# Gate and up of a SwiGLU layer, token-stationary, with a fast matrix product on part of the contraction

## The chip, the core and the metric

The kernel runs on one core of a Trainium2 chip. Five engines work side by side, each through its own queue of instructions in order: TensorE (PE, matrix products), VectorE (DVE), ScalarE (ACT), GpSimd (POOL) and SyncE (SP, which issues the weight transfers here). The metric is the device time of one execution, in microseconds (us).

## What is computed

A decoder trunk of two layers over 256 tokens (2 token tiles of 128) with a model width of 2048 (16 k-tiles of 128). Each layer has a mixer of three head groups, which the change doesn't touch, and a SwiGLU feed-forward part (FFN) of width 5632 = 44 x 128:

```python
def rms_norm(x, w):
    y = xf * lax.rsqrt(jnp.mean(xf * xf, axis=-1, keepdims=True) + NORM_EPS)
    return (y * w.astype(jnp.float32)).astype(x.dtype)

def swiglu(h, w_gate, w_up, w_down):
    return (jax.nn.silu(h @ w_gate) * (h @ w_up)) @ w_down

for l in range(DEPTH):
    h = rms_norm(x, mix_norm_w[l])
    x = x + hybrid_mixer(h, ...)
    h = rms_norm(x, ffn_norm_w[l])
    x = x + swiglu(h, w_gate[l], w_up[l], w_down[l])
return rms_norm(x, final_norm_w)
```

All data are float32.

## The kernel before

**Products in three parts.** Every float32 operand is split into a high part (rounded to the matmul's own format) and the rest, the low part. A product a x b is then three matmuls: high x high, high x low and low x high. For a weight tile, `unit` (lines 125 to 136) does it: SP brings a unit of 128 x 1024 values (512 KB) into one of three `raw` buffers, ACT writes the high part `whi` (line 134), DVE subtracts it from the raw values to give `wlo` (line 135). `whi` and `wlo` have four buffers each. The activations lie transposed as x^T: `hs[k]` holds for k-tile k a tile `hl` of 512 columns, 256 tokens high and 256 tokens low.

**Two forms of a product.** `block_a` (line 162) holds the weights still and moves the tokens: for each k-tile one matmul of `whi` against all 512 columns of `hl`, then one of `wlo` against the 256 high columns. The result is transposed (FFN column by token) and sits in two halves that `evac_a` (line 178) adds. `block_b` (line 186) holds a token tile still and moves 512 weight columns: three matmuls of 512 columns for each k-tile and token tile.

**The FFN** (`ffn`, line 804). It runs in three parts of 16, 16 and 12 tiles of 128 FFN columns (`FF_PARTS`). For each tile f `block_a` computes gate (`pg`) and up (`pu`); ACT and DVE join the halves, multiply both by `rb` (the row of 1/rms of each token, broadcast over the partitions), take Silu and multiply (lines 815 to 820); the result is split into `hid` high and low. After the tiles of a part `block_b` runs the down product (`dn`) over that part's tiles for each of four groups of 512 output columns, and `add_x` adds it to x. In the last part each finished group of columns starts what comes next (`nxt.piece`): the transposes of x and their split for the next layer's mixer, or the squares and weights of the final norm, which ends with `Final.last` for one token tile after the other. x^T is not scaled before the products: 1/rms is applied to the result, so the first products needn't wait for it.

**What sets the order.** A scheduler of the framework places each engine's instructions by its own timeline; tiles from a pool with n buffers wait until an old one is free. PSUM, where products end, has 8 banks of 512 columns: four for `dps` (tag "d"), two for tag "m" and two for "mg". The DVE row for weights is the plainest piece of it:

```python
act.activation(out=whi[:, c], in_=raw[:, c], func=AF.Copy)
dve.tensor_tensor(out=wlo[:, c], in0=raw[:, c], in1=f32(whi[:, c]), op=SUB)
```

Of the kernel before, what the change touches and what calls it, by code (L numbers as in the profile page):

```python
# [58 lines left out]
def tile_trunk(ctx: ExitStack, tc: tile.TileContext, x: bass.AP, wu: bass.AP, prm: bass.AP,  # L59
               cst: bass.AP, fnw: bass.AP, out: bass.AP, depth: int, units: list):  # L60
    nc = tc.nc
# [116 lines left out]
    def evac_a(ps, dst, rb, scale=None):  # L178
        act.copy(out=dst, in_=ps[:, S:])  # L179
        dve.tensor_tensor(out=dst, in0=ps[:, :S], in1=dst, op=ADD)  # L180
        if scale is None:
            dve.tensor_tensor(out=dst, in0=dst, in1=rb, op=MUL)
        else:
            dve.scalar_tensor_tensor(out=dst, in0=dst, scalar=scale, in1=rb, op0=MUL, op1=MUL)
# [617 lines left out]
            dve.tensor_tensor(out=xc, in0=pst[t][:, :w], in1=xc, op=ADD)  # L802

    def ffn(l, norm, nxt):
        hs = norm.hs
        rb = None
        f0 = 0
        for part, nf in enumerate(FF_PARTS):
            fs = []
            for f in range(f0, f0 + nf):  # L810
                pg, pu = dps("pg"), dps("pu")
                block_a(l, (("gate", f * P, pg), ("up", f * P, pu)), hs)
                if rb is None:
                    rstd, rb = norm.scale()
                ga = sp.tile([P, S], F32, tag="ac", name="ga", bufs=2)
                evac_a(pg, ga, rb)
                act.activation(out=ga, in_=ga, func=AF.Silu)
                up = sp.tile([P, S], F32, tag="tz", name="up", bufs=2)
                evac_a(pu, up, rb)
                dve.tensor_tensor(out=up, in0=up, in1=ga, op=MUL)  # L820
                if f % 2 == 0:
                    hid = g4("hid", [2, 2, S], F32R, "gg" if part % 2 else "gy")
                hi, lo = hid[:, 0, f % 2], hid[:, 1, f % 2]
                act.activation(out=hi, in_=up, func=AF.Copy)  # L824
                dve.tensor_tensor(out=lo, in0=up, in1=f32(hi), op=SUB)  # L825
                fs.append((hi, lo))
# [101 lines left out]
```

## Time and profile before

| | us |
|---|---|
| median of 3 runs (2394.24 to 2395.49) | 2394.96 |
| the profiled execution | 2394.46 |
| its span, first to last instruction | 2392.7 |
| PE busy | 2377.5 (99%) |
| DVE busy | 1498.8 (63%) |
| ACT busy | 1197.6 (50%) |
| POOL busy | 75.7 (3%) |

The profile is of one execution; its times are compared with that execution's own 2394.46 us. Matmuls are pipelined: the next begins before the record of the last ends, so the pitch from one to the next, not the mean duration, says what one costs. The chain that ended last is followed back from the last instruction, at each step to what released it.

### The profile page before, as it was taken

The numbers are of one execution on the slowest core, as the hardware profiler recorded it, in microseconds if no ns is written. First come the engines' busy times: TensorE is split into PE (matmuls) and PEld (weight loads), VectorE is DVE, ScalarE is ACT, GpSimd is POOL, SyncE is SP. The second block draws the span as 40 slices with busy tenths as digits, with TensorE's granted clock in tenths as the row PEclk, the third lists the DMA queues.
The fourth block names the chain that finished last, engine by engine and source line by source line (L and its number), as shares of the span: only waits on it lengthen the run. The fifth ranks groups of instructions, "written<-read, shape, count | busy, mean of one in ns | idle before, by whom it ended". The sixth has DMA issues, their size and how long they took to land.

```text
span 2392.7 us, 34536 instructions
## 1 busy us (share of the span) xinstructions
PE 2377.5 (99%) x13300; PEld 2075.5 (87%) x13300; DVE 1498.8 (63%) x2354; ACT 1197.6 (50%) x1875; POOL 75.7 (3%) x107
## 2 busy tenths in 40 slices
PE   8999999999999999999999999999999999999998
PEld 7888888888888888888898888889888888888887
DVE  5898655566655665466658976565666556655665
ACT  5754455555434454444567545555554344544544
POOL 0220000000000000000003100000000000000000
PEclk9999999999999999999999999999999999999999
DMA  6555445455565555556555544454656655566564
GB/s 214 174 176 167 136 159 187 162 191 195 194 195 176 196 192 197 189 178 197 190 172 184 176 145 155 159 185 160 196 194 196 194 177 189 196 206 194 184 202 159
DMA packets 120886, 436.06 MB, mean 182 GB/s; under 512 B 13584, under 2 KB 14480, under 8 KB 120720
## 3 DMA queue, kind: packets, MB, share of 16 engines
q1 hardware_dynamic: 120160, 432.70, 55.5%
q8 instruction: 104, 1.70, 0.3%
q10 hardware_dynamic: 560, 1.15, 0.1%
q14 instruction: 62, 0.51, 0.1%
HBM read 431.70 MB, written 2.10 MB: 181 GB/s over the span
## 4 chain that ended last, share of the span: by engine, by line
PE 98%; DMA 1%; ACT 1%; DVE 0%; issue 0%; POOLq 0%; POOL 0%; DVEq 0%; ACTq 0%
PE pu L69 20%; PE pg L69 20%; PE dn L69 20%; PE wo L69 7%; PE fq L69 4%; PE fk L69 4%; PE fv L69 4%; PE gkq L69 3%; PE mq L69 2%; PE mk L69 2%; PE gvp L69 2%; PE gz L69 2%; PE mv L69 2%; PE mo L69 1%; PE fs L69 1%; PE mog L69 1%
## 5 line engine op out<-in xcount | busy, mean ns | idle before, releaser
L135 DVE TENSOR_TENSOR wlo<-raw,whi 128x1024 fp32r<-128x1024 f32 (+2 forms) x821 | 991.0, 1218 | 658.8 <-ACT whi L134 432.1
L134 ACT ACTIVATE whi<-raw 128x1024 fp32r<-128x1024 f32 (+2 forms) x821 | 866.4, 1056 | 869.5 <-DMA raw<-wu 448.5
L69 PE MATMUL dn<-whi,hid 128*128 128x512 f32 (+1 forms) x1504 | 440.6, 376 | 0.0
L69 PE MATMUL pu<-hl,whi 128*128 128x512 f32 x1408 | 350.2, 391 | 0.0
L69 PE MATMUL pg<-hl,whi 128*128 128x512 f32 x1408 | 336.9, 391 | 0.0
L69 PEld LDWEIGHTS dn<-whi,hid 128*128 128x128 f32 x1504 | 276.2, 188 | 50.6
L69 PEld LDWEIGHTS pu<-hl,whi 128*128 128x128 f32 x1408 | 259.0, 188 | 50.3
L69 PEld LDWEIGHTS pg<-hl,whi 128*128 128x128 f32 x1408 | 259.0, 188 | 50.2
L69 PE MATMUL dn<-wlo,hid 128*128 128x512 f32 (+1 forms) x752 | 282.6, 376 | 0.0
L69 PEld LDWEIGHTS pg<-hl,wlo 128*128 128x128 f32 x1408 | 191.0, 190 | 13.1
L69 PE MATMUL pg<-hl,wlo 128*128 128x256 f32 x1408 | 195.1, 282 | 0.0
L69 PE MATMUL pu<-hl,wlo 128*128 128x256 f32 x1408 | 183.3, 283 | 0.0
L69 PEld LDWEIGHTS pu<-hl,wlo 128*128 128x128 f32 x1408 | 175.4, 192 | 0.2
L69 PE MATMUL wo<-whi,yhl 128*128 128x512 f32 (+1 forms) x640 | 169.3, 350 | 0.0
L69 PEld LDWEIGHTS dn<-wlo,hid 128*128 128x128 f32 x752 | 141.6, 188 | 25.7
L69 PEld LDWEIGHTS wo<-whi,yhl 128*128 128x128 f32 x640 | 112.6, 189 | 14.7
L69 PE MATMUL wo<-wlo,yhl 128*128 128x512 f32 (+1 forms) x320 | 111.7, 349 | 0.0
L179 ACT COPY up<-pu 128x256 f32<-128x256 f32 x88 | 32.9, 373 | 123.8 <-PE pu L69 123.8
L825 DVE TENSOR_TENSOR hid<-up,hid 128x256 fp32r<-128x256 f32 x88 | 37.4, 425 | 82.9 <-ACT hid L824 82.9
L69 PE MATMUL fv<-whi,hl 128*128 128x512 f32 x256 | 83.0, 398 | 0.0
L69 PE MATMUL fk<-hl,whi 128*128 128x512 f32 x256 | 67.9, 402 | 0.0
L69 PEld LDWEIGHTS wo<-wlo,yhl 128*128 128x128 f32 x320 | 60.6, 189 | 7.2
(318 smaller groups left out, 2512.4 us busy)
## 6 DMA issues: line engine op xcount, KB each, us to landing
raw<-wu SPq DMA_DIRECT2D x808, 512.0 KB, 4.2
raw<-wu SPq DMA_DIRECT2D x10, 420.0 KB, 3.1
xall<-x SPq DMA_DIRECT2D x3, 512.0 KB, 8.5
fw<-fnw SPq DMA_DIRECT2D x2, 512.0 KB, 5.3
out<-xall ACTq DMA_DIRECT2D x2, 512.0 KB, 3.0
out<-xall SPq DMA_DIRECT2D x2, 512.0 KB, 3.0
xall<-x SPq DMA_DIRECT2D x2, 256.0 KB, 4.4
raw<-wu SPq DMA_DIRECT2D x2, 140.0 KB, 2.5
```

Of the source, the lines that this page charges most:

```text
L69: self.log.append(nc.tensor.matmul(*a, **k).ins)
L134: act.activation(out=whi[:, c], in_=raw[:, c], func=AF.Copy)
L135: dve.tensor_tensor(out=wlo[:, c], in0=raw[:, c], in1=f32(whi[:, c]), op=SUB)
L179: act.copy(out=dst, in_=ps[:, S:])
L825: dve.tensor_tensor(out=lo, in0=up, in1=f32(hi), op=SUB)
```

## The change

**Token-stationary.** Gate and up are computed for blocks of 512 FFN columns: token tiles stand still, weights move, and the result has tokens on partitions. It is transposed on PE afterwards (`hT`, 8 transposes a block) and split into `hid`.

**A fast product for some k-tiles.** The values wanted are G0, G1 (gate of token tile 0 and 1) and U0, U1 (up). For two k-tiles together they are a 2 x 2 matrix product of blocks, which takes 8 products in the plain way and 7 in Strassen's (in Winograd's form). `PAIRS = (3, 11)` names the k-tiles 3 and 4, and 11 and 12, that are treated so (`quad`); the other 12 go the plain way with 4 products (`plain`), with one difference: U0 is had as a product with the difference of the two token tiles, so that it can be added to what the quads give. Seven PSUM banks p1 to p7 take the seven products; sums of them make G0, G1, U0 and U1. `quad` fetches two units into their own buffers `rq`, and makes the sums and differences of their blocks on DVE and POOL in place; ACT and DVE split them into `th` and `tl`.

**x^T scaled.** Sums of activations are needed as operands (`sd`, also split), and the seven results mix, so the 1/rms has to be in the operands. The first block of a layer (`slow`) runs without the fast product, scales its results afterwards, and `normalise` then rewrites x^T in place and makes the sums. The other ten blocks are `fast`.

**Six parts** of 2, 2, 2, 2, 2 and 1 blocks (8, 8, 8, 8, 8 and 4 tiles) in place of 16, 16 and 12. The tag "m" becomes two tags of one bank each, m0 and m1.

```diff
-FF_PARTS = (16, 16, 12)
+FF_PARTS = (2, 2, 2, 2, 2, 1)
+PAIRS = (3, 11)
...
+        def hilo(e, v):
+            act.activation(out=e[:, 0], in_=v, func=AF.Copy)
+            dve.tensor_tensor(out=e[:, 1], in0=v, in1=f32(e[:, 0]), op=SUB)
+            return e[:, 0], e[:, 1]
+
+        def normalise(rb):
...
+            for k in range(KT):
+                hi, lo, hl = hs[k]
+                y[k % 2] = yk = sp.tile([P, S], F32, tag="ac", name="yn", bufs=2)
+                pool.tensor_tensor(out=yk, in0=f32(hi), in1=f32(lo), op=ADD)
+                dve.tensor_tensor(out=yk, in0=yk, in1=rb, op=MUL)
+                act.activation(out=hi, in_=yk, func=AF.Copy)
+                dve.tensor_tensor(out=lo, in0=yk, in1=f32(hi), op=SUB)
+                if k - 1 in PAIRS:
...
+                    pool.tensor_tensor(out=s1, in0=y0[:, P:], in1=yk[:, P:], op=ADD)
+                    pool.tensor_tensor(out=s2, in0=s1, in1=y0[:, :P], op=SUB)
+                    pool.tensor_tensor(out=s4, in0=yk[:, :P], in1=s2, op=SUB)
+                    for n, v in (("s1", s1), ("s2", s2), ("s4", s4)):
+                        ops[n, k - 1] = hilo(free.pop(), v)
+                else:
...
+                    pool.tensor_tensor(out=v, in0=yk[:, :P], in1=yk[:, P:], op=SUB)
+                    ops["d", k] = hilo(free.pop(), v)
+
+        def quad(c, k):
...
+                nc.sync.dma_start(out=rq[i], in_=wu[u].rearrange("p (a b) -> p a b", a=2))
+            b12, b11, b22, b21 = (rq[i][:, j] for i in range(2) for j in range(2))
...
+            dve.tensor_tensor(out=b11, in0=b12, in1=b11, op=SUB)
+            pool.tensor_tensor(out=b12, in0=b22, in1=b12, op=SUB)
+            dve.tensor_tensor(out=b22, in0=b22, in1=b11, op=SUB)
+            pool.tensor_tensor(out=b21, in0=b21, in1=b22, op=SUB)
+            for hi, lo, v in zip(th, tl, rq):
+                act.activation(out=hi, in_=v, func=AF.Copy)
+                dve.tensor_tensor(out=lo, in0=v, in1=f32(hi), op=SUB)
...
+            t3, t1, t2, t4 = ((th[i][:, j], tl[i][:, j]) for i in range(2) for j in range(2))
+            return ((1, half(k, 0), cols(w0, 0)), (2, half(k + 1, 0), cols(w1, 1)), (3, ops["s4", k], cols(w1, 0)),
+                    (5, ops["s1", k], t1), (7, ops["d", k], t3), (6, ops["s2", k], t2), (4, half(k + 1, 1), t4))
+
+        def plain(c, k):
+            whi, wlo = unit(("s", l, "ug", c, k, 1, 1024))
+            up, gate = ((whi[:, j * 512:(j + 1) * 512], wlo[:, j * 512:(j + 1) * 512]) for j in range(2))
+            return (2, half(k, 0), gate), (4, half(k, 1), gate), (5, half(k, 1), up), (3, ops["d", k], up)
+
+        def fast(c, first):
...
+                    pe.matmul(ps[i], ahi, whi, start=i not in seen, stop=False)
+                    pe.matmul(ps[i], ahi, wlo, start=False, stop=False)
+                    pe.matmul(ps[i], alo, whi, start=False, stop=end)
...
+                if k == PAIRS[-1]:
+                    act.copy(out=xs[:, 0], in_=ps[1])
+                    dve.tensor_tensor(out=xs[:, 1], in0=ps[6], in1=xs[:, 0], op=ADD)
+                    dve.tensor_tensor(out=ys[:, 0], in0=ps[7], in1=xs[:, 1], op=ADD)
+            for t, i, v in ((0, 2, xs[:, 0]), (1, 4, ys[:, 0])):
+                dve.tensor_tensor(out=ga[:, t], in0=ps[i], in1=v, op=ADD)
+                act.activation(out=ga[:, t], in_=ga[:, t], func=AF.Silu)
+            dve.tensor_tensor(out=ys[:, 1], in0=ps[5], in1=xs[:, 1], op=ADD)
+            dve.tensor_tensor(out=ys[:, 0], in0=ps[5], in1=ys[:, 0], op=ADD)
+            dve.tensor_tensor(out=ys[:, 1], in0=ps[3], in1=ys[:, 1], op=ADD)
+            for t in range(2):
+                dve.tensor_tensor(out=ga[:, t], in0=ga[:, t], in1=ys[:, 1 - t], op=MUL)
+
+        def slow(c):
+            pg = [dps("pg") for t in range(2)]
+            block_b(l, "gate", c, pg, hs, 0, KT, True, True)
+            rstd, rb = norm.scale()
+            for t in range(2):
+                act.activation(out=ga[:, t], in_=pg[t], func=AF.Silu, scale=rstd[:, t:t + 1])
+            pu = [dps("pu") for t in range(2)]
+            block_b(l, "up", c, pu, hs, 0, KT, True, True)
...
+            normalise(rb)
...
+                        for t in range(2):
+                            pe.transpose(ps[:, i * S + t * P:i * S + (t + 1) * P],
+                                         ga[:, t, (q + i) * P:(q + i + 1) * P], ident)
+                    hid = g4("hid", [2, 512], F32R, "gy")
+                    act.copy(out=hid[:, 0], in_=ps)
+                    dve.tensor_tensor(out=hid[:, 1], in0=ps, in1=f32(hid[:, 0]), op=SUB)
```

How the instructions then stand shows best at three places. DVE, at the start of layer 0's FFN, before: the weight splits with the join of the halves between them.

```order
L244 TENSOR_REDUCE s_4789<-ssq 128x2
L224 TENSOR_SCALAR rstd<-s_4789 128x2
L220 SCALAR_TENSOR_TENSOR hl<-xT,pr,hl 128x256 x2
L135 TENSOR_TENSOR wlo<-raw,whi 128x1024 x2
L180 TENSOR_TENSOR ga<-pg,ga 128x256
L135 TENSOR_TENSOR wlo<-raw,whi 128x1024
L182 TENSOR_TENSOR ga<-ga,rb 128x256
L180 TENSOR_TENSOR up<-pu,up 128x256
```

Behind the last `hl` come only weight splits and work on results; nothing rewrites x^T.

DVE, now, in the slow block, from the first tile of the scaling on (`yn` is x^T joined again, `hl` its new low part, `sd` the low part of a sum):

```order
L842 TENSOR_TENSOR yn<-yn,rb 128x256 x2
L141 TENSOR_TENSOR wlo<-raw,whi 128x1024
L844 TENSOR_TENSOR hl<-yn,hl 128x256 x2
L830 TENSOR_TENSOR sd<-dt,sd 128x128 x2
L842 TENSOR_TENSOR yn<-yn,rb 128x256
L141 TENSOR_TENSOR wlo<-raw,whi 128x1024
L842 TENSOR_TENSOR yn<-yn,rb 128x256
L844 TENSOR_TENSOR hl<-yn,hl 128x256
L830 TENSOR_TENSOR sd<-dt,sd 128x128
```

Between two weight splits there now stand four or five small operations of the scaling. This goes on for the 16 tiles, past the end of the slow block and through the first quad.

POOL around the same place, before: small things of the mixer, and of the FFN nothing but the power of its norm (`rstd`).

```order
L374 MEMSET mv 128x8
L448 MEMSET bm 128x384
L225 TENSOR_TENSOR rf<-rf,mhalf 128x8
L225 TENSOR_TENSOR rstd<-rstd,mhalf 128x2
L382 MEMSET gtk 128x256
```

No weight and no x^T passes over POOL.

POOL, now, some way on, where layer 0's first quad begins (`dt` is the difference of the two token tiles, `st` the three sums of a pair, `rq` a unit of the quad):

```order
L856 TENSOR_TENSOR dt<-yn 128x128 x2
L841 TENSOR_TENSOR yn<-hl 128x256
L874 TENSOR_TENSOR rq<-rq 128x512
L841 TENSOR_TENSOR yn<-hl 128x256
L856 TENSOR_TENSOR dt<-yn 128x128
L876 TENSOR_TENSOR rq<-rq 128x512
L849 TENSOR_TENSOR st<-yn 128x128
L850 TENSOR_TENSOR st<-st,yn 128x128
L851 TENSOR_TENSOR st<-yn,st 128x128
```

POOL now joins each k-tile of x^T, makes 18 sums of 128 columns a layer for the operands, and the first sums of a quad stand between them.

PE, at the end of a layer's last part, before: the last products of `pu`, then `dn`, which begins with older tiles of the part.

```order
L69 MATMUL pg<-hl,wlo 128x256 x10
L69 MATMUL pu<-hl,wlo 128x256 x16
L69 MATMUL dn<-whi,hid 128x512 x2
L69 MATMUL dn<-wlo,hid 128x512
L69 MATMUL dn<-whi,hid 128x512
```

`dn` follows `pu` directly.

PE, now (`p_9672` is p3 of the last block; its products with `sd` are the last of the block):

```order
L70 MATMUL p_9678<-whi,hl 128x512
L70 MATMUL p_9678<-wlo,hl 128x512
L70 MATMUL p_9678<-whi,hl 128x512
L70 MATMUL p_9672<-whi,sd 128x512
L70 MATMUL p_9672<-wlo,sd 128x512
L70 MATMUL p_9672<-whi,sd 128x512
L73 MATMUL hT<-ident,ga 128x128 x4
L70 MATMUL dn<-whi,hid 128x512
L70 MATMUL dn<-wlo,hid 128x512
```

The transposes `hT` of the block just computed stand between its last product and the first of `dn`.

DVE there, now, in the last block of layer 1 (p_19737 and p_19738 are p2 and p4, p_19739 is p5, p_19733 is p3):

```order
L915 TENSOR_TENSOR ga<-p_19737,pa 128x512
L141 TENSOR_TENSOR wlo<-raw,whi 128x1024
L915 TENSOR_TENSOR ga<-p_19738,pb 128x512
L141 TENSOR_TENSOR wlo<-raw,whi 128x1024
L917 TENSOR_TENSOR pb<-p_19739,pa 128x512
L918 TENSOR_TENSOR pb<-p_19739,pb 128x512
L141 TENSOR_TENSOR wlo<-raw,whi 128x1024
L919 TENSOR_TENSOR pb<-p_19733,pb 128x512
L921 TENSOR_TENSOR ga<-ga,pb 128x512 x2
L952 TENSOR_TENSOR hid<-hT,hid 128x512 x2
```

Splits of weights for `dn` stand between the sums that make the block's gate and up.

## Rows read from the trace of the kernel before

**Rows 1.** The page, part 1: busy us, share of the span, instructions.

```profile
PE 2377.5 (99%) x13300; PEld 2075.5 (87%) x13300; DVE 1498.8 (63%) x2354; ACT 1197.6 (50%) x1875; POOL 75.7 (3%) x107
```

**Rows 2.** Page part 4, the chain; then PE's longest wait: us, times, longest.

```profile
PE pu L69 20%; PE pg L69 20%; PE dn L69 20%; PE wo L69 7%; PE fq L69 4%; PE fk L69 4%; PE fv L69 4%; PE gkq L69 3%; PE mq L69 2%; PE mk L69 2%; PE gvp L69 2%; PE gz L69 2%; PE mv L69 2%; PE mo L69 1%; PE fs L69 1%; PE mog L69 1%
...
PE mv L69 <- ACT hl L219: 2.9, 2, 2.6
```

**Rows 3.** The chain in order of time, 630 to 735: start us, us, what.

```profile
635.72 3.65 PE pg L69 x16
...
646.85 87.07 PE dn L69 x384
```

**Rows 4.** Timeline of PE, 1153 to 1155: start us, us, instruction.

```profile
1153.34 0.39 PE L69 MATMUL dn<-whi,hid 128*128 128x512 f32 x1
1153.58 0.38 PE L72 MATMUL xT<-ident,xall 128*128 128x128 f32 x2
1153.71 0.48 PE L69 MATMUL dn<-whi,hid 128*128 128x512 f32 x1
1154.03 0.82 PE L72 MATMUL xT<-ident,xall 128*128 128x128 f32 x6
1154.60 0.48 PE L69 MATMUL dn<-wlo,hid 128*128 128x512 f32 x1
```

**Rows 5.** Groups by form, DVE and ACT: busy us, mean ns, idle before.

```profile
L135 DVE TENSOR_TENSOR wlo<-raw,whi 128x1024 fp32r<-128x1024 f32 x807 | 978.4, 1223 | 641.7 <-ACT whi L134 415.1 <-PE pg L69 210.1 <-PE fq L69 3.4
...
L820 DVE TENSOR_TENSOR up<-up,ga 128x256 f32<-128x256 f32 x88 | 36.8, 418 | 1.1 <-ACT ga L817 1.0
...
L802 DVE TENSOR_TENSOR xall<-dn,xall 128x512 f32<-128x512 f32 x44 | 28.2, 682 | 0.0
...
L714 DVE TENSOR_TENSOR mo<-mn,mo 128x128 f32<-128x128 f32 x16 | 3.7, 281 | 0.0
...
L355 ACT ACTIVATE fv<-fv,rstd 128x512 f32<-128x512 f32 x8 | 5.5, 690 | 3.9 <-PE fv L69 3.9
```

**Rows 6.** POOL: its only sum of two tensors, durations in ns (min/median/max).

```profile
L498 POOL TENSOR_TENSOR ac<-ac,tz x24: 730/744/1653, 80.8 to 1335.2; 128x256 f32<-128x256 f32 x24
```

**Rows 7.** Timeline of DVE and POOL at three places in the mixer.

```profile
79.86 0.48 DVE L496 SCALAR_TENSOR_TENSOR ac<-xc,pr,ac 128x256 f32<-128x256 f32 x1
80.26 0.48 DVE L497 SCALAR_TENSOR_TENSOR tz<-xc,pr,tz 128x256 f32<-128x256 f32 x1
...
80.82 0.91 POOL L498 TENSOR_TENSOR ac<-ac,tz 128x256 f32<-128x256 f32 x1 [1.49 <-DVE tz L497]
81.05 0.96 DVE L497 SCALAR_TENSOR_TENSOR tz<-xc,pr,tz 128x256 f32<-128x256 f32 x1
...
88.20 1.87 POOL L495 TENSOR_SCALAR tz<-xc,pr 128x256 f32<-128x256 f32 x2 [5.33 <-DVE xc L182]
88.37 0.58 DVE L182 TENSOR_TENSOR xc<-xc,rb 128x256 f32<-128x256 f32 x1
...
126.13 0.74 POOL L498 TENSOR_TENSOR ac<-ac,tz 128x256 f32<-128x256 f32 x1
126.19 0.70 DVE L527 TENSOR_TENSOR nk<-gss,gr 128x8 f32<-128x8 f32 x1
...
126.81 0.15 DVE L531 TENSOR_TENSOR br<-col,gr 128x8 f32<-128x8 f32 x1
```

**Rows 8.** Windows: us; busy PE, PEld, DVE, ACT, POOL; PEclk; DMA, GB/s.

```profile
9.00:12.00 3.00, 3.00 (x12) 2.43 (x11) 2.25 (x5) 2.48 (x6) 0.00 (x0) 0.61 1.03 401
12.00:15.00 3.00, 3.00 (x13) 2.00 (x12) 2.96 (x8) 2.15 (x8) 0.00 (x0) 0.82 1.05 405
```

**Rows 9.** Timeline of DVE at the program's end.

```profile
2380.76 0.42 DVE L802 TENSOR_TENSOR xall<-dn,xall 128x256 f32<-128x256 f32 x1 [2.56 <-PE dn L69]
...
2382.70 0.52 DVE L320 TENSOR_SCALAR xall<-xall,frstd 128x576 f32<-128x576 f32 x1 [0.66 <-POOL frstd L225]
...
2385.07 0.42 DVE L802 TENSOR_TENSOR xall<-dn,xall 128x256 f32<-128x256 f32 x1 [1.13 <-PE dn L69]
```

More of the change, by code (lines that the diff above doesn't have):

```diff
@@ L805, in ffn @@
         hs = norm.hs
-        rb = None
+        rstd = None
         f0 = 0
-        for part, nf in enumerate(FF_PARTS):
-            fs = []
[L810 to L826, printed above, removed]
+        th, tl = ([g4(n, [2, 512], F32R) for i in range(2)] for n in ("th", "tl"))
@@ new lines, in ffn, with half @@
+        sd = [g4("sd", [4, 2, P], F32R) for i in range(5)]
+        rq = [g4("rq", [2, 512], tag="gd") for i in range(2)]
+        xs, ys = (g4(n, [2, 512], tag="gd") for n in ("pa", "pb"))
+        ga = g4("ga", [2, 512], tag="gd")
+        ops = {}
+        def half(k, t):
+            return hs[k][0][:, t * P:(t + 1) * P], hs[k][1][:, t * P:(t + 1) * P]
+        def hilo(e, v):
+            act.activation(out=e[:, 0], in_=v, func=AF.Copy)
+            dve.tensor_tensor(out=e[:, 1], in0=v, in1=f32(e[:, 0]), op=SUB)
+            return e[:, 0], e[:, 1]
@@ new lines, in quad, with cols @@
+        def quad(c, k):
+            for i in range(2):
+                u = len(units)
+                units.append(("s", l, "ug", c, k + i, 1, 1024))
+                nc.sync.dma_start(out=rq[i], in_=wu[u].rearrange("p (a b) -> p a b", a=2))
+            b12, b11, b22, b21 = (rq[i][:, j] for i in range(2) for j in range(2))
+            w0, w1 = ([wp.tile([P, 1024], F32R, tag=n, name=n) for n in ("whi", "wlo")] for i in range(2))
+            act.activation(out=w0[0][:, :512], in_=b11, func=AF.Copy)
+            dve.tensor_tensor(out=w0[1][:, :512], in0=b11, in1=f32(w0[0][:, :512]), op=SUB)
+            r1 = rq[1].rearrange("p a b -> p (a b)")
+            act.activation(out=w1[0], in_=r1, func=AF.Copy)
+            dve.tensor_tensor(out=w1[1], in0=r1, in1=f32(w1[0]), op=SUB)
+            dve.tensor_tensor(out=b11, in0=b12, in1=b11, op=SUB)
[5 more added lines that the diff above has]
+                dve.tensor_tensor(out=lo, in0=v, in1=f32(hi), op=SUB)
+            def cols(w, j):
+                return tuple(v[:, j * 512:(j + 1) * 512] for v in w)
+            t3, t1, t2, t4 = ((th[i][:, j], tl[i][:, j]) for i in range(2) for j in range(2))
+            return ((1, half(k, 0), cols(w0, 0)), (2, half(k + 1, 0), cols(w1, 1)), (3, ops["s4", k], cols(w1, 0)),
+                    (5, ops["s1", k], t1), (7, ops["d", k], t3), (6, ops["s2", k], t2), (4, half(k + 1, 1), t4))
@@ new lines, in plain @@
+        def plain(c, k):
[3 more added lines that the diff above has]
+        def fast(c, first):
+            ps = {3: dps("p3")}
+            for i in ((1, 6, 7) if first else (2, 4, 5)):
+                ps[i] = dps(f"p{i}")
+            for i, tag in zip((2, 4, 5) if first else (6, 7, 1), ("mg", "mg", "m1")):
+                ps[i] = mps(f"p{i}", tag)
+            seen = set()
+            for k in range(KT):
+                if k - 1 in PAIRS:
+                    continue
+                for i, (ahi, alo), (whi, wlo) in quad(c, k) if k in PAIRS else plain(c, k):
+                    end = k == KT - 1 or (i in (1, 6, 7) and k == PAIRS[-1])
+                    pe.matmul(ps[i], ahi, whi, start=i not in seen, stop=False)
+                    pe.matmul(ps[i], ahi, wlo, start=False, stop=False)
+                    pe.matmul(ps[i], alo, whi, start=False, stop=end)
+                    seen.add(i)
+                if k == PAIRS[-1]:
[10 more added lines that the diff above has]
+                dve.tensor_tensor(out=ga[:, t], in0=ga[:, t], in1=ys[:, 1 - t], op=MUL)
@@ new lines, in ffn @@
+        for part, blocks in enumerate(FF_PARTS):
+            nf = 4 * blocks
+            fs = []
+            for c in range(f0 * P, (f0 + nf) * P, 512):
+                if c == 0:
+                    slow(c)
+                else:
+                    fast(c, c == 512 or c == f0 * P)
+                for q in range(0, 4, 2):
+                    ps = mps("hT", "m0")
+                    for i in range(2):
+                        for t in range(2):
+                            pe.transpose(ps[:, i * S + t * P:i * S + (t + 1) * P],
[3 more added lines that the diff above has]
+                    dve.tensor_tensor(out=hid[:, 1], in0=ps, in1=f32(hid[:, 0]), op=SUB)
+                    fs += [(hid[:, 0, i * S:(i + 1) * S], hid[:, 1, i * S:(i + 1) * S]) for i in range(2)]
```

20 lines of the change are left out of this document (18 added, 2 removed).

## The prediction

> **What bounds the kernel now.** I read the page's busy shares first, then the chain that ended last, then that chain in order of time, and last the forms of DVE, ACT and POOL. PE is busy for 2377.5 of 2392.7 us [rows 1]. The chain runs along PE: its gate and up (`pu`, `pg`) hold 20% each, `dn` another 20%, and the longest wait of PE in the whole program is 2.6 us, at its very start [rows 2]. So an FFN microsecond is a matmul microsecond: only fewer or cheaper matmuls shorten it, and anything that lets PE run dry lengthens it. In order of time one tile of 128 FFN columns takes 646.85 - 635.72 = 11.13 us, and the down stage follows with no gap, 384 products of 512 columns in 87.07 us, 226.7 ns each [rows 3]. An 11.13 us step is 32 such products at 3.65/16 = 228 ns and 32 of 256 columns, which get the rest, 3.83/32 = 120 ns: more than half of 228. DVE is at 63%, ACT at 50%, POOL at 3%; all three have room on average, and the question is whether they have it in the stretches where the change puts its work.
>
> **What PE is spared.** Four steps make a block of 512 columns: 44.53 us now. Token-stationary, all products are 512 wide: 2 matrices x 16 k-tiles x 2 token tiles x 3 = 192, 43.5 us. In a fast block two pairs of k-tiles take 7 x 3 instead of 8 x 3 products, so 186, 42.2 us. There are 22 blocks, 2 of them slow (192) and 20 fast: 384 + 3720 = 4104 products x 226.7 ns = 930.4 us against 88 x 11.13 = 979.4. New on PE are 8 transposes `hT` a block. The like ones (`xT`) stand between two products at 1153.34 and the third at 1154.60: 1.26 us for two products and eight transposes, so 0.10 us each [rows 4], and 176 of them cost 17.8 us. PE's own work falls by 979.4 - 930.4 - 17.8 = **31.2 us**. The weights loaded are the same bytes; the mixer's instructions stand in the same order; ACT's and DVE's old evacuations (six 256-wide DVE operations a tile) give way to nine 512-wide ones a block. All that lies off the path as long as PE is fed.
>
> **What feeds PE, and the port.** In a fast block DVE has 12 + 2 `wlo` of 1.22 us, 4 `tl` of 1.22, and 17 operations of 512 columns at 0.68 (two half `wlo`, four sums of operands, nine evacuations, two `hid`): 33.5 us by the means of [rows 5]. POOL has four sums of 512 columns. The only POOL sum of two tensors in the trace is 256 wide, 0.744 us [rows 6]; 512 columns cost between that and twice that, and I take 1.35, near the double, since most of such a time should go with the columns. What such a sum does to DVE is in the trace: the same DVE form takes 0.48 us alone and 0.96 when it starts beside POOL's sum, and a DVE operation on 8 columns, 0.15 elsewhere, takes 0.70, until the sum is over [rows 7]. So a DVE operation that reads two tensors from SBUF and a POOL sum don't overlap; `wlo`, `tl`, `lo` and the sums are all of that kind. A POOL operation with one tensor holds DVE up far less: 0.58 instead of the 0.42 of [rows 5] beside an operation of 0.93 us [rows 7]. A fast block then asks DVE and POOL together for 33.5 + 4 x 1.35 = 38.9 us, and PE takes 42.2 + 0.8. It fits, with 4 us to spare. In a second block of a part (8 of them) the evacuation of the block before is queued ahead of the first quad, and my count of its steps comes out within half a microsecond of PE's need: 8 x 0.4 = **3 us**, from 0 to 20.
>
> [...] With full blocking the next term would be 15 us a layer and the time 2419; with the small delay for every POOL operation it would be 0.2 and the time about 2388.
>
> **The slow block and the scaling (the largest cost).** `normalise` rewrites all 16 tiles of x^T while the slow block's `up` half runs and the first fast block begins. Per tile: a POOL sum, a DVE product with `rb`, ACT's `hi`, DVE's `lo`, then differences on POOL, each split again by ACT and DVE. `rb` comes some 4.0 us after `up` begins, since ACT does two `Silu` of the gate first. From there until the second `tl` of the first quad, DVE's row holds 29 operations of 256 columns, 18 of 128, 7 of 512 and 14 of 1024: 29 x 0.42 + 18 x 0.28 + 7 x 0.68 + 14 x 1.22 = 39.1 us by the means of [rows 5]; DVE starts the next about 0.08 us before the record of the last ends (0.40 between starts of 0.48 us operations, [rows 7]), so 33.7 us packed. POOL has 13 sums of 256 columns, 18 of 128 and 2 of 512 in that stretch. A 128-wide one costs at most the 0.744 of a 256-wide one [rows 6]; half of that would be 0.37, if all of it went with the columns, and I take 0.45. That is 9.7 + 8.1 + 2.7 = 20.5 us, of which DVE is held for all but the last 0.14 of each [rows 7]: 15.9. PE's work from the start of `up` to the products that want that `tl` is 185 products and 8 transposes, 42.8 us. So 4.0 + 33.7 + 15.9 = 53.6 comes 10.8 us late; POOL, DVE and ACT also wait for each other tile by tile, for which I add 1.2. **12 us a layer, 24 in all.** Ends: 0 (POOL holds nothing) and 20.8 (means unpacked, whole POOL durations) a layer. Behind the late `tl` queue the next `wlo`, so the ring of four weight tiles doesn't rescue PE.
>
> **The last block of a layer.** Before, the last part had 12 tiles and PE went from its last `pu` straight to products of older tiles. Now the sixth part is one block, and nothing older is left: every `dn` product wants a `hid` of this block. After the last product DVE's row (in the section on the change) still holds two `wlo` between the sums, two sums of p5, that of p3 and two multiplications: 2 x 1.22 + 5 x 0.68 = 5.8 us, of which some 0.6 run before it; then 4 transposes 0.4, ACT's copy of 512 columns 0.69 [rows 5], and hops between engines of about 0.5. **7 us a layer, 14 in all**; 3.5 without the two `wlo`, 9 if more queue. The other parts have the first block's half of `dn` (24 products, 5.4 us) as cover; I charge them nothing, and without it each of the ten would cost about as much again.
>
> **The clock.** [...] Two drains: **3.4 us**; 0 to 10 with the scaling's gaps.
>
> **The ends.** At the very end the two token tiles' tails start 2385.07 - 2380.76 = 4.3 us apart, filled by 36 products; now 12 products lie between, 1.4 us, so the first tile's scaling (2382.70 on) stands before the second's on DVE [rows 9]: about 1.8 us, and as much for DVE's weight multiplications, squeezed from 12 tiles of cover into 4: **3.5 us**, 1 to 6. Layer 0's end squeezes the transposes of x likewise, but the next stage's first products cover it: **1 us**, 0 to 3.
>
> **The sum**, against the profiled execution's 2394.46 us (its span 2392.7 and 1.8 around it; the median of the runs is 2394.96, 0.5 more, which I neglect): 2394.5 - 31.2 + 3 + 24 + 14 + 3.4 + 3.5 + 1 = **2412 us**, 0.7% slower.
>
> **Rivals.** (1) The scaling hides: POOL's pieces fall where DVE waits anyway, and the drains come out short: 2394.5 - 31.2 + 2 + 7 + 1 = 2373, up to 2388 with a few us a layer. For it: DVE at 63%, and packed DVE alone fits into the 38.8 us. It decides below 5 us a layer with drains of 4. Against it: eight doubled DVE operations of one kind. (2) DVE becomes the bound in every fast block: if each quad's `tl` waits for POOL and ACT in DVE's row for more than 2 us, the 4 us to spare are gone; 2 us over, 20 times, is 40 on the forecast, 2452. (3) The saving is smaller than it reads: with products at the 228 ns of [rows 3], 4104 x 1.3 ns = 5 us more. That is in the range.
>
> **How the numbers follow.** Forecast 0.53, its own range 2398 to 2432; rival 1 0.25, rival 2 0.12; 0.10 for mixtures that land within 0.2% (4.8 us, about what runs of this kernel can tell from no change). Faster 0.25, same 0.11, slower 0.64. Range 2378 to 2438: below it lies the lower end of rival 1, above it rival 2, together 0.2.
>
> **What would show it.** Right: PE waits 10 us or more a layer in one place, right after the slow block, for `wlo` and `tl` of DVE, with POOL `yn` and `dt` beside and DVE operations stretched by up to a POOL duration; a gap of 7 us before the first `hT` of each layer's last block; fast blocks later on at 43 us. Wrong: first fast block as quick as the others (rival 1), or all of them at 45 us (rival 2), or `up` products not at 227 ns.

## The result, and the profile after

The changed kernel takes 2416.7 us (median of 4 runs, 2414.82 to 2416.89) against 2394.74 us before: a ratio of 1.0091, 95% interval 1.0078 to 1.0103. It is 22 us slower; the prediction was 2412, slower, with a range of 2378 to 2438. The profiled execution has a span of 2414.6 us.

The page of the changed kernel, busy shares, and of its chain the shares by engine and by line; they answer to [rows 1, 2]:

```profile
PE 2368.0 (98%) x11852; PEld 1995.4 (83%) x11852; DVE 1680.2 (70%) x2366; ACT 1212.0 (50%) x1783; POOL 278.3 (12%) x259
...
PE 88%; DVE 4%; issue 2%; ACT 2%; DMA 2%; POOL 1%; POOLq 0%; DVEq 0%; SPq 0%; ACTq 0%
PE p L70 31%; PE dn L70 19%; PE wo L70 7%; PE fq L70 4%; PE fk L70 4%; PE fv L70 4%; PE gkq L70 3%; PE mv L70 2%; DMA raw<-wu 2%; PE mq L70 2%; PE mk L70 2%; PE gvp L70 2%; PE gz L70 2%; PE pg L70 2%; DVE wlo L141 1%
```

PE is busy for 9.5 us less, and yet 12% of the chain now runs over something else than PE. PE's own waits (engine, line, waited for: us in total, times, longest) say where; before, the wait at the program's start (`mv`) was the longest:

```profile
PE hT L73 <- DVE ga L921: 12.3, 6, 5.8
PE p L70 <- DVE wlo L141: 7.1, 5, 2.9
...
PE p L70 <- DVE tl L879: 1.6, 2, 0.8
```

Of the 12.3, 11.6 are two drains of 5.8 us, one at each layer's last block; `wlo` and `tl` are late in each layer's first fast block. The chain in order of time (start us, us, what) gives the pace of the rest, as [rows 3] did before:

```profile
611.23 51.01 PE p L70 x225
...
741.69 51.01 PE p L70 x225
...
872.46 51.01 PE p L70 x225
...
1003.24 51.00 PE p L70 x225
...
1133.52 40.13 PE p L70 x177
```

Within a block a product costs 51.01/225 = 226.7 ns, as in [rows 3]. A part of two fast blocks with its down products takes 130.3 to 130.8 us in layer 0, where 564 such products and 16 transposes make 129.5.

The first place, in layer 0's first fast block (timeline: start us, us, engine, instruction, idle before):

```profile
523.68 1.26 POOL L874 TENSOR_TENSOR rq<-rq 128x512 f32<-128x512 f32 x1
523.75 1.49 DVE L842 TENSOR_TENSOR yn<-yn,rb 128x256 f32<-128x256 f32 x1 [1.05 <-POOL yn L841]
...
526.75 1.21 DVE L141 TENSOR_TENSOR wlo<-raw,whi 128x1024 fp32r<-128x1024 f32 x1
...
528.01 0.65 PE L70 MATMUL p<-wlo,hl 128*128 128x512 f32 x1 [2.92 <-DVE wlo L141]
...
536.12 1.50 DVE L879 TENSOR_TENSOR tl<-rq,th 128x1024 fp32r<-128x1024 f32 x1
...
540.05 1.22 DVE L879 TENSOR_TENSOR tl<-rq,th 128x1024 fp32r<-128x1024 f32 x1
...
542.78 0.39 PE L70 MATMUL p<-tl,sd 128*128 128x512 f32 x1
```

DVE first waits 1.05 us for POOL's `yn`, then its multiplication takes 1.49 us (0.42 in [rows 5]) beside POOL's 1.26 us sum, and the `wlo` for which PE stands still is queued behind all that. The two `tl` are those of the first quad; PE waits for the first (one of the two waits of 0.8 us above) and not for the second. The second place, layer 0's last block (PE and DVE of the timeline):

```profile
1175.29 0.39 PE L70 MATMUL p<-whi,sd 128*128 128x512 f32 x1
...
1176.02 1.22 DVE L141 TENSOR_TENSOR wlo<-raw,whi 128x1024 fp32r<-128x1024 f32 x1
...
1177.15 0.69 DVE L917 TENSOR_TENSOR pb<-p,pa 128x512 f32<-128x512 f32 x1
1177.75 0.68 DVE L918 TENSOR_TENSOR pb<-p,pb 128x512 f32<-128x512 f32 x1
1178.35 1.22 DVE L141 TENSOR_TENSOR wlo<-raw,whi 128x1024 fp32r<-128x1024 f32 x1
1179.48 0.69 DVE L919 TENSOR_TENSOR pb<-p,pb 128x512 f32<-128x512 f32 x1
1180.08 1.29 DVE L921 TENSOR_TENSOR ga<-ga,pb 128x512 f32<-128x512 f32 x2
...
1181.52 1.09 PE L73 MATMUL hT<-ident,ga 128*128 128x128 f32 x4 [5.84 <-DVE ga L921]
...
1183.28 0.79 PE L70 MATMUL dn<-whi,hid 128*128 128x512 f32 x1 [0.67 <-ACT hid L951]
```

The two `wlo` between the sums are those of the order shown ahead of the prediction. From the last product's end at 1175.29 + 0.23 to the first `dn` pass 7.8 us. The windows around both places in both layers (us; PE busy, PEld, DVE, ACT, POOL; granted clock; DMA share, GB/s), to be held against [rows 8]:

```profile
490.00:538.00 48.00, 41.41 (x174) 31.85 (x174) 43.76 (x65) 28.49 (x56) 31.58 (x34) 0.96 0.45 149
525.00:535.00 10.00, 5.82 (x19) 3.69 (x18) 10.00 (x13) 6.78 (x13) 8.43 (x9) 0.83 0.30 100
1720.00:1730.00 10.00, 6.65 (x18) 4.20 (x18) 10.00 (x13) 6.36 (x13) 8.43 (x10) 0.66 0.26 81
1180.00:1190.00 10.00, 7.81 (x28) 6.09 (x29) 2.75 (x5) 1.72 (x3) 0.00 (x0) 0.66 0.23 67
2375.00:2385.00 10.00, 6.48 (x19) 5.04 (x20) 3.49 (x6) 1.17 (x2) 0.00 (x0) 0.50 0.32 103
```

From the start of `up` to the end of the first quad's first `tl`, DVE is busy for 43.76 of 48 us and POOL for 31.58. In the four shorter windows the granted clock is 0.83, 0.66, 0.66 and 0.50, with a wait of PE of 2.9 us (the first two) or 5.8 us (the others) in them or reaching into them. Where it is 0.50 the `dn` products stand 0.43 us apart (1184.29, 1184.72, 1185.15), for 0.23 where it is 1.00.

### The profile page after: what moved, and what is told of

It reads as the page before. It is cut to its first block, busy times and chain, and to the rows that moved or that the text cites. A ratio compares the mean times of both kernels' runs of the same rounds, so it can differ in the third digit from the quotient of the medians.

```text
span 2414.6 us, 31866 instructions
## 1 busy us (share of the span) xinstructions
PE 2368.0 (98%) x11852; PEld 1995.4 (83%) x11852; DVE 1680.2 (70%) x2366; ACT 1212.0 (50%) x1783; POOL 278.3 (12%) x259
## 4 chain that ended last, share of the span: by engine, by line
PE 88%; DVE 4%; issue 2%; ACT 2%; DMA 2%; POOL 1%; POOLq 0%; DVEq 0%; SPq 0%; ACTq 0%
PE p L70 31%; PE dn L70 19%; PE wo L70 7%; PE fq L70 4%; PE fk L70 4%; PE fv L70 4%; PE gkq L70 3%; PE mv L70 2%; DMA raw<-wu 2%; PE mq L70 2%; PE mk L70 2%; PE gvp L70 2%; PE gz L70 2%; PE pg L70 2%; DVE wlo L141 1%
## 5 line engine op out<-in xcount | busy, mean ns | idle before, releaser
L141 DVE TENSOR_TENSOR wlo<-raw,whi 128x1024 fp32r<-128x1024 f32 (+3 forms) x741 | 918.7, 1247 | 473.5 <-ACT whi L140 455.0
L140 ACT ACTIVATE whi<-raw 128x1024 fp32r<-128x1024 f32 (+3 forms) x741 | 775.8, 1053 | 772.2 <-PE dn L70 244.3
L70 PE MATMUL p<-whi,hl 128*128 128x512 f32 x1600 | 546.6, 391 | 1.0 <-ACT whi L140 1.0
L70 PEld LDWEIGHTS p<-whi,hl 128*128 128x128 f32 x1600 | 301.3, 188 | 63.5 <-ACT whi L140 1.9
L70 PE MATMUL p<-wlo,hl 128*128 128x512 f32 x800 | 313.2, 392 | 7.1 <-DVE wlo L141 7.1
L70 PE MATMUL p<-whi,sd 128*128 128x512 f32 x560 | 216.3, 391 | 0.0
L70 PEld LDWEIGHTS p<-wlo,hl 128*128 128x128 f32 x800 | 150.5, 188 | 41.0 <-DVE wlo L141 9.8
L874 POOL TENSOR_TENSOR rq<-rq 128x512 f32<-128x512 f32 x40 | 57.4, 1436 | 989.5 <-DVE rq L873 973.7
L70 PEld LDWEIGHTS p<-whi,sd 128*128 128x128 f32 x560 | 105.9, 189 | 21.6
L70 PE MATMUL p<-wlo,sd 128*128 128x512 f32 x280 | 109.8, 392 | 0.0
L876 POOL TENSOR_TENSOR rq<-rq 128x512 f32<-128x512 f32 x40 | 83.1, 2078 | 120.5 <-DVE rq L875 117.4
L871 DVE TENSOR_TENSOR wlo<-rq,whi 128x1024 fp32r<-128x1024 f32 x40 | 56.1, 1401 | 52.9 <-ACT whi L870 52.8
```

Source lines behind the costliest of these rows:

```text
L70: self.log.append(nc.tensor.matmul(*a, **k).ins)
L871: dve.tensor_tensor(out=w1[1], in0=r1, in1=f32(w1[0]), op=SUB)
L874: pool.tensor_tensor(out=b12, in0=b22, in1=b12, op=SUB)
L876: pool.tensor_tensor(out=b21, in0=b21, in1=b22, op=SUB)
```

## The experiments

Theory at the start: each layer loses some 12 us where the scaling starves PE, since POOL's sums hold DVE, and 8 us where a lone last block drains. All runs are compared with 2416.7 us of the changed kernel; before took 2393.7 to 2394.1 us beside them.

**Without the scaling.** `normalise` is not called; unscaled halves of x^T stand in for its sums, so the number of products stays.

```diff
-            normalise(rb)
+            for k in range(KT):
+                if k - 1 in PAIRS:
+                    ops["s1", k - 1], ops["s2", k - 1], ops["s4", k - 1] = half(k, 0), half(k, 1), half(k, 0)
+                else:
+                    ops["d", k] = half(k, 0)
```

> Leaves out the scaling of x^T and the sums of its tiles: the operands sd are replaced by unscaled halves of x^T, so the number of products stays as it is. The changed kernel's first part of each layer (slow block, first fast block, their down products) takes 143.7 us against 130.8 for its products and transposes at the pitch of before, 12.9 too many. Theory (the scaling starves PE): both layers lose 11 to 12 of these, 2416.7 - 23 = 2394 us (2391 to 2397). Rival (the change of form from slow to fast block costs it: the first quad's chain over POOL, the transposes between): 2408 or more.

Measured 2394.8 us, as the theory had it. The scaling costs 21.9 us, 11 a layer; the change of form from slow to fast block costs next to nothing.

**Its sums on DVE.** `pool.tensor_tensor` becomes `dve.tensor_tensor` in all five places of `normalise`: 16 sums of 256 columns a layer and 20 of 128 (14 `dt` and 6 `st`; the 18 of the text ahead of the result and of the expectation miss two).

> All sums of the scaling go from POOL to DVE, 16 of 256 and 18 of 128 columns a layer; nothing is left out. Theory (while POOL sums two tensors DVE is held, so POOL's help is none): DVE gets some 13 x 0.34 + 18 x 0.20 = 8.0 us of work up to the first quad's second tl and is rid of 11.8 us by which its operations there are stretched and of 4.8 us in which it waits: 8 us less a layer, 2416.7 - 16 = 2401 us (2396 to 2408). Rival (DVE is simply too full there, and POOL takes work off it): 8 us more a layer, 2433 us.

Measured 2415.4 us: neither. One group by form (busy us, mean ns, idle before), from 490 to 538 us, of the changed kernel and then of this one, and this one's window:

```profile
L830 DVE TENSOR_TENSOR sd<-dt,sd 128x128 fp32r<-128x128 f32 x11 | 6.4, 593 | 0.0
```

```profile
L830 DVE TENSOR_TENSOR sd<-dt,sd 128x128 fp32r<-128x128 f32 x13 | 3.6, 288 | 0.0
...
490.00:538.00 48.00, 42.36 (x178) 33.21 (x177) 45.20 (x104) 27.80 (x54) 5.70 (x2) 0.94 0.49 159
```

With 2 POOL operations in place of 34 in this window `sd` takes 288 ns, near the 281 of [rows 5], but DVE has 104 operations instead of 65 in the same 48 us and is as full as before. POOL's help is worth nothing here, and taking it away gains nothing either. PE now waits for `th`, the high part of a quad's sums (its wait: us in total, times, longest; then POOL and ACT of the timeline):

```profile
PE p L70 <- ACT th L878: 9.1, 3, 4.4
...
519.80 2.14 POOL L876 TENSOR_TENSOR rq<-rq 128x512 f32<-128x512 f32 x1 [0.87 <-DVE rq L875]
...
532.65 1.04 ACT L878 ACTIVATE th<-rq 128x1024 fp32r<-128x1024 f32 x1
```

The last of the quad's sums is ready at 521.94, yet `th` runs 10.7 us later: in ACT's row it stands behind splits of the scaling.

**The lone block first**, and **the lone block fifth.**

```diff
-FF_PARTS = (2, 2, 2, 2, 2, 1)
+FF_PARTS = (1, 2, 2, 2, 2, 2)
```

> Parts of 1, 2, 2, 2, 2, 2 blocks in place of 2, 2, 2, 2, 2, 1: the block that stands alone is the slow one. Theory: the 7.8 us drain at the end of layer 0 and the 12.0 us by which layer 1's last part is too long (drain, slow clock, squeezed tail) go, about 18 us; the lone slow block gets a drain of some 5 us before its first dn; its 96 dn products (21.8 us, in which DVE has 8 wlo and 8 additions, 15.2 us) give the scaling 6.6 us of room. 2416.7 - 18 + 10 - 13 = 2396 us (2385 to 2404). Rival (a lone block's drain costs the same wherever it stands, and the scaling stays late by as much): only the tail's 4 us come back, 2412 us.

```diff
-FF_PARTS = (2, 2, 2, 2, 2, 1)
+FF_PARTS = (2, 2, 2, 2, 1, 2)
```

> Parts of 2, 2, 2, 2, 1, 2 blocks: the lone block is a fast one in the middle. Theory (every dn product of a lone fast block waits for this block's own sums, transposes and splits): the drain of 7 to 8 us a layer is still there, in the middle, and only the squeezed tail of layer 1 and the start of layer 1's mixer come back, 4 to 5 us: 2412 us (2409 to 2414). Rival (what costs is the end of a layer, where the squares, transposes and splits of x meet the last block's sums): 16 to 20 us come back, 2398 us.

Measured 2395.4 and 2413.1 us, both as the theory had it. In the second, PE still waits 5.8 us twice, now in the middle: the drain belongs to a lone fast block, not to the end of a layer. In the first the drain sits at the slow block:

```profile
PE hT L73 <- DVE ga L932: 13.5, 4, 6.6
```

Its two evacuations (0.7 us each) stand in DVE's row behind the scaling of tiles that nobody wants yet. That suggests the next two.

**Scaling held back.** From k-tile 6 (or 8) on, x^T is multiplied with a copy of `rb` that depends on the slow block's `ga`; parts as in the run with the lone block first.

```diff
-                dve.tensor_tensor(out=yk, in0=yk, in1=rb, op=MUL)
+                dve.tensor_tensor(out=yk, in0=yk, in1=rb if k < 6 else late, op=MUL)
...
+            dve.scalar_tensor_tensor(out=late, in0=ga[:, 1, :S], scalar=0.0, in1=rb, op0=MUL, op1=ADD)
...
```

> As the run with parts of 1, 2, 2, 2, 2, 2, and the scaling of k-tiles 6 to 15 is multiplied with a copy of rb that needs the slow block's finished ga, so DVE cannot put it ahead of the slow block's own two evacuations (one small DVE operation a layer more). In the run without this, the second half of the lone slow block and its down products took 30.8 + 24.5 us a layer, 10.9 more than 192 products and 8 transposes; PE waited 6.7 us of it for ga. Theory (the wait is DVE's row: scaling queued ahead of ga; part of it is work that only moves behind): the wait falls to 2 us, ten tiles of the scaling, some 19 us of DVE with what POOL holds of it, move beside dn, where not all fit: 2395.4 less 2 x 2 to 2 x 6 us, 2388 us (2382 to 2392). Rival (DVE's sum of work up to the first quad is the bound, so the order within it is worth nothing): 2395 us, PE's wait then stands at the first fast block.

> The same with k-tiles 8 to 15 held back: two tiles more, about 4 us of DVE with what POOL holds, stand ahead of the slow block's evacuations. Theory: the wait for ga is 2 to 4 us longer than with 6 to 15 held back, and if nothing is late at the first fast block then the time is 4 to 8 us above that run's; if that run is late there, the two are within 2 us. Rival (order worth nothing): 2395 us as well.

Measured 2386.0 us (ratio to before 0.9969, interval 0.9958 to 0.9980) and 2396.5 us. With 6 the wait is down to 4.9 us in all and next to nothing is late afterwards:

```profile
PE hT L73 <- DVE ga L932: 4.9, 4, 2.2
```

With 8 it is 11.3 us in all, not far from the 13.5 of the run that holds nothing back. So the order of DVE's row, not only its sum, decides; two tiles are worth 10 us over both layers, more than the 4 to 8 expected. The wait is 6.4 us longer, and the mean granted clock of the profiled execution is lower, 0.995 in place of 0.997.

**What of POOL costs the time.** Three kernels keep DVE's and ACT's operations and change POOL's. First, operations with one tensor in place of the sums (low parts and second operands left out).

```diff
-                pool.tensor_tensor(out=yk, in0=f32(hi), in1=f32(lo), op=ADD)
+                pool.tensor_scalar(out=yk, in0=f32(hi), scalar1=1.0, scalar2=None, op0=MUL)
...
```

> The changed kernel, with POOL's sums of the scaling replaced by products of one tensor with 1.0 in the same places (the low parts of x^T and the second operands of the sums are left out). The one-input form of 256 columns took 0.93 us in the trace of before, the sum 0.74, so POOL has as much to do or more. Theory (a sum of two tensors holds DVE, an operation on one tensor hardly): DVE's operations up to the first quad's second tl are stretched by some 2 us in place of 11.8, and the first part of each layer is 8 to 12 us shorter: 2398 us (2392 to 2402). Rival (the hops from POOL to DVE to ACT and back, tile by tile, cost the time, not the port): no gain, 2414 us or more.

Measured 2413.4 us: next to the rival (what it calls the port is the hold of POOL's sums on DVE), 3.3 us less than the changed kernel. The groups of 490 to 538 us, of the changed kernel and of this one:

```profile
L842 DVE TENSOR_TENSOR yn<-yn,rb 128x256 f32<-128x256 f32 x15 | 9.3, 629 | 1.1 <-POOL yn L841 1.1
...
L841 POOL TENSOR_TENSOR yn<-hl 128x256 f32<-128x256 f32 x13 | 11.3, 879 | 2.4 <-DVE hl L844 2.4
```

```profile
L842 DVE TENSOR_TENSOR yn<-yn,rb 128x256 f32<-128x256 f32 x16 | 8.1, 526 | 0.0
...
L830 DVE TENSOR_TENSOR sd<-dt,sd 128x128 fp32r<-128x128 f32 x14 | 5.3, 399 | 1.0 <-ACT sd L829 1.0
L841 POOL TENSOR_SCALAR yn<-hl 128x256 f32<-128x256 f32 x14 | 14.8, 1069 | 0.8 <-DVE hl L844 0.8
```

About half of DVE's stretching is gone (`sd` 593 to 399 ns, undisturbed 288), yet the time hardly moves, while POOL's steps are longer (1.07 us for 0.88). DVE's second `tl` now ends 46.5 us after `up` began (489.19 to 535.65), 4.9 us sooner than in the changed kernel, but PE waits for `th`:

```profile
PE p L70 <- ACT th L878: 4.5, 4, 1.8
```

So the hold of DVE alone is not the cause. The second kernel leaves POOL out altogether (x^T is scaled from its high part alone, and halves of it stand in for the sums of 128 columns); the third is the same with a MEMSET of three columns where each sum stood, of which the diff shows one.

```diff
-                pool.tensor_tensor(out=yk, in0=f32(hi), in1=f32(lo), op=ADD)
-                dve.tensor_tensor(out=yk, in0=yk, in1=rb, op=MUL)
+                pool.memset(yk[:, :3], 0.0)
+                dve.tensor_tensor(out=yk, in0=f32(hi), in1=rb, op=MUL)
...
```

> The changed kernel with the scaling's POOL operations left out (x^T is scaled from its high part alone, and plain halves of it take the place of the 18 sums of a layer), DVE and ACT with the same operations as before. Theory A (POOL's sums make the scaling late, by the 11.8 us for which they stretch DVE and by their own time in its row of dependent steps; DVE's own 37.4 us up to the first quad's second tl would fit): the first part of each layer loses 2 to 4 us in place of 12.9: 2397 us (2393 to 2402). Theory B (DVE's own work is what doesn't fit there): 2410 us or more.

> As the run without POOL, but where each sum stood POOL now sets three columns to zero (0.10 us as in the mixer), so that every step from DVE to POOL and on to ACT or DVE is still there, with next to no time on POOL and nothing that holds DVE. If the steps between engines cost the time: 2408 us or more. If only POOL's own time and its hold on DVE cost it: within 3 us of the run without POOL, 2397 us.

Measured 2395.7 and 2408.2 us. Without POOL PE isn't late at all in this stretch (its window: 48.00 of 48.00 busy). With steps that take 0.1 us, beside which DVE's `yn` and `hl` take 417 and 418 ns (629 and 474 in the changed kernel), more than half of the loss is back:

```profile
490.00:538.00 48.00, 48.00 (x216) 39.44 (x215) 41.35 (x79) 31.59 (x61) 5.92 (x2) 1.00 0.55 182
...
519.55 1.06 ACT L872 ACTIVATE th<-rq 128x1024 fp32r<-128x1024 f32 x1 [1.52 <-POOL rq L868]
```

```profile
490.00:538.00 48.00, 44.84 (x196) 36.05 (x195) 39.76 (x74) 29.30 (x58) 7.13 (x36) 0.96 0.55 182
...
496.33 0.10 POOL L854 MEMSET yn<- 128x3 f32 x1 [25.24 <-DVE hl L844]
...
498.54 0.30 POOL L841 MEMSET yn<- 128x3 f32 x2 [1.72 <-DVE sd L830]
...
529.23 0.75 ACT L843 ACTIVATE hl<-yn 128x256 fp32r<-128x256 f32 x2 [2.01 <-DVE yn L842]
...
530.71 1.04 ACT L876 ACTIVATE th<-rq 128x1024 fp32r<-128x1024 f32 x1
```

DVE is less busy there than in the run without POOL and PE waits all the same: the first `th` of the quad stands in ACT's row behind splits that wait for later tiles, and starts 11 us later. Leaving POOL's part out gives back 21.0 us, cutting its steps to 0.1 us only 8.5. The 12.5 between the two are not the price of the changed kernel's own steps: here the MEMSET that stands for a sum writes into `yn`, so it waits for DVE's `hl`, and the first MEMSET of a later tile for `sd`, which still reads the same buffer. The changed kernel's `dt` waits for the product `yn` alone. The order of the rows differs too from that of the run without POOL. What is shown is that the chain and its order can keep PE waiting although POOL's steps take next to no time.

**Token-stationary alone.** All 22 blocks are slow, with no scaling.

```diff
-            normalise(rb)
...
-                if c == 0:
-                    slow(c)
-                else:
-                    fast(c, c == 512 or c == f0 * P)
+                slow(c)
...
```

> Token-stationary gate and up in all 22 blocks with neither the fast product nor the scaling, parts as in the changed kernel; nothing is left out. Theory: 120 products more (27.2 us), no scaling (minus 23 us), the drain at each layer's end shorter since only two evacuations stand behind the last product (minus 2 to 3 us a layer): 2416.7 + 27 - 23 - 5 = 2416 us (2411 to 2419), so the fast product earned some 4 us net. Rival (fast blocks cost PE something beside the scaling, port and DVE in every block): 2408 us or less.

Measured 2399.0 us (1.0021 of before, interval 1.0012 to 1.0030): the rival, for a reason that I had priced too low (the drains) and one that I had not priced (the second blocks of a part). The last block here:

```profile
1173.58 1.40 DVE L935 SCALAR_TENSOR_TENSOR ga<-pu,rstd,ga 128x512 f32<-128x512 f32 x2
...
1174.38 0.33 PE L73 MATMUL hT<-ident,ga 128*128 128x128 f32 x1 [0.35 <-DVE ga L935]
...
1176.26 0.50 PE L70 MATMUL dn<-whi,hid 128*128 128x512 f32 x1 [0.68 <-ACT hid L950]
```

Its drain hardly exists, since gate is done before `up` ends and only two operations are left. And its parts take 132.48 us for 576 products and 16 transposes (132.2), 0.3 over, where the fast ones are 0.8 to 1.9 over 129.5. The last parts take 70.4 and 78.4 us, those of the changed kernel 75.9 and 84.8 with 6 products (1.4 us) less. So the fast product saves 120 x 0.2267 = 27.2 us and costs 21.9 for the scaling, 6.9 + 7.8 for the longer drains and 7.5 in eight parts: 17 net, of a difference of 17.7.

**Two slow blocks.** The first part is slow as a whole and the scaling runs beside its down products; the last part has three blocks, or all but the first have.

```diff
-FF_PARTS = (2, 2, 2, 2, 2, 1)
+FF_PARTS = (2, 2, 2, 2, 3)
...
-            normalise(rb)
+            if c == 512:
+                normalise(rb)
...
-                if c == 0:
+                if c <= 512:
...
```

> Parts of 2, 2, 2, 2, 3 blocks, and the first two blocks of a layer are slow ones, so that the whole first part is unscaled; x^T is rewritten during the second block's up half and its part's down products, and no block stands alone. 6 products more a layer, 2.7 us in all. Theory (the scaling needs some 22 us of DVE that the down products of two blocks, 43.5 us with 27.7 us of DVE work, and the up half before them can give): no drain, no late scaling: 2394.5 - 31.2 + 2.7 for the products, and 1.1 us for each of 10 parts of 2 as the changed kernel shows beyond them: 2377 us (2374 to 2384). Rival (the scaling still ends after the down products, or holds up the evacuation of the second slow block): 2390 us or more.

> The same with parts of 2, 3, 3, 3 blocks: one turn from a part's products to its down products and back, and 8 additions to x, fewer a layer. Theory (a part's turn costs some 1 us): 2 us less than with parts of 2, 2, 2, 2, 3. Rival (the cost lies in each block's evacuation, not in the turn): the same within 1 us.

Measured 2386.0 us (0.9969, 0.9958 to 0.9981) and 2383.8 us (0.9959, 0.9947 to 0.9972): faster than both kernels, though 9 us above the forecast, so that the first is neither the theory (2374 to 2384) nor the rival (2390 or more). In both of them PE still waits once a layer for a `wlo` behind the scaling, in the first part's down products:

```profile
PE dn L70 <- DVE wlo L141: 3.6, 2, 1.8
```

With parts of three, layer 0's products behind that wait stand 0.43 us apart (566.40, 566.83, 567.25), for 0.23 before it. The first part's down products take 49.7 to 51.3 us in place of the 44.5 of the plain parts. Parts of three give 2.2 us more, as expected, but the two intervals overlap, so that this difference is not shown.

## Why the prediction was right

The direction, the size and the two places were right; the way in which the larger one comes about was right only in part.

- **What PE is spared:** right. 226.7 ns a product held in the new form; rival 3 (228 ns) falls. The sum should have had 1.3 us more on this side: in each layer the shorter last part has 96 fewer halves of 256 columns, which is worth 0.6 us.
- **The scaling, 12 us a layer:** the sum was right, the path to PE was not. The 185 products and 8 transposes from the start of `up` (489.96) to the first product with the second `tl` (542.78) take 52.8 us for 42.8: 10 us late, where I had 10.8. (The two values beside it were estimates from [rows 7]: 15 us with POOL's whole durations, 20.5 for 15.9; 0.2 us with 0.58 - 0.42 = 0.16 us for each of 33 POOL operations.) DVE's row was nearly as forecast: that `tl` ends at 541.27, 51.3 us after `up` began, for 53.6. Against the means of [rows 5], DVE's operations are stretched by 11.7 us in this row, for 15.9, and DVE idles for 1.5 us in it, for the 1.2 that I charged for engines waiting for each other. But PE isn't late for this `tl`. Its waits come before, above all for `wlo` and the first `tl`, 6.6 us in all between 510 and 540, spread and not in one place as I had listed, and the lower clock (0.83 from 525 to 535) adds to them. And where DVE's row is shorter, PE waits for another: with one input for `th` in ACT's row, which I had priced at nothing. This is the step that failed: I took the end of DVE's row as what PE waits for. For the whole first part, `pg` at 467.32 to the second part at 611.23, the loss is 12.2 us: 143.9 less 130.8 for 570 products and 16 transposes, and less 0.9 for eight small products that the kernel before has too. In layer 1 it is 12.0, and without the scaling 1.2 in the same stretch. That 12 came out so exactly is in part luck: by DVE's row alone PE would be 8.5 late, and the slow clock and 1.5 us of waiting in the down products make up the rest.
- **The last block, 7 us:** right, 7.8 with the lower clock in it. The 0.5 for hops between engines was an estimate that no row gave; between the records of `ga`, `hT`, ACT's `hid` and `dn` lie 0.15, 0.03 and 0.06 us, while the four transposes take 1.09 us at a granted clock of 0.50, for 0.4. The two `wlo` stand where the order had them, and the run with the lone block fifth shows the same 5.8 us of waiting elsewhere.
- **The clock, 3.4 us:** too low. No run shows this term: it takes for each drain the 3 x 0.39 + 3 x 0.18 = 1.7 us that the granted clocks of [rows 8] give for the program's start, an estimate. What the traces show is a granted clock of 0.50 for 3.4 us at that start, for 6.8 us at layer 0's last block (1180.2 to 1186.9) and for 10.2 us at layer 1's (2374.8 to 2385.0), and also for 3.4 and 6.8 us inside the first fast blocks (528.2 to 531.6, 1722.9 to 1729.7). By the windows shown, what was lost is at most (1 - 0.83) x 10 + (1 - 0.66) x 10 + 3.4 + 5.0 = 13.5 us, less what PE waited in them anyway: some 10 us, an estimate. They lie in the 12 and 7.8 above, so that the waits themselves were shorter than forecast.
- **The second blocks, 3 us:** too low. Eight parts of two fast blocks are 0.8 to 1.9 us above 129.5, 9.9 us in all, and no single wait in them is above 0.9 us; the plain parts are 0.3 above theirs.
- **The ends:** right. Layer 1's last part, 2329.85 to the end, is 8.8 us longer than layer 0's; before, the like difference was 4.7: 4.1 us against 3.5, though some of it is the clock, which is lower behind layer 1's drain (0.50) than behind layer 0's (0.66). Layer 0's end: the next mixer takes 453.3 us (1209.44 to 1662.76) for 451.9, 1.4 against 1.
- **Rivals:** 1 (the scaling hides) falls with the first experiment; 2 (DVE the bound in every fast block) with 130.5 us a part.

Open: what share of the scaling's 11 us a layer is POOL's hold on DVE, the time of a step between engines, the two buffers of `yn` that let only two tiles be under way, or the order that the scheduler then writes. The kernels that change POOL's part have different orders in DVE's and ACT's rows, so their differences are not those of one cost alone. In the three of them in which PE is late, the first quad's `th` runs some 9 to 11 us after the last of the quad's sums; in the run without POOL it stands earlier, and PE isn't late. The same operations with `th` put first, or with more buffers of `yn`, weren't tried.

## What to carry to other kernels

A form of a product that needs prepared operands is paid where the preparation meets the first use, and where the last evacuation has nothing beside it; price those two places before the products saved, and lay out the stages so that each has older work of PE as cover (here 33 us between the changed kernel and the one with two slow blocks and parts of three, which even has 12 products more). Work that nobody waits for yet can stand in an engine's row ahead of work that is wanted (ACT's `th` ran 10.7 us after its sum was ready); a false dependency that holds such work back was worth 9 us here. A chain of small steps shared between DVE, POOL and ACT can keep PE waiting although no engine's busy time explains it (with POOL's steps cut to 0.1 us, DVE was busy for 39.8 of 48 us and PE for 44.8): look at what stands in each row ahead of the step that PE wants.
